# Sums over the partitions for sub-norm and modulation: ones stationary on four column groups and a turn, in place of one-column products

## The chip, the cores and the metric

The kernel runs on one core of a Trainium2 chip. The metric is the device time of one execution in microseconds (us): the median of three runs. Before the change it is 1350.98 us (the three runs span 1350.11 to 1352.2 us).

The engines have short names in all rows: PE is TensorE (PEld its loads of the stationary operand, which run ahead of the products), DVE is VectorE, ACT is ScalarE, POOL is GpSimd, SP is SyncE, which issues the DMA transfers. A PE product has a stationary operand (up to 128x128) and a moving operand whose columns stream through; its sum over the partitions lands in PSUM.

## The reference

The kernel computes two layers of a transformer block in float32 for 512 latent tokens `x` (width 1024), with 256 context tokens `ctx` that layer 0 reads. Cut to what matters here:

```python
for i in range(2):                                   # layer 0: diff_attention, layer 1: short_conv
    mod = silu(c) @ ada_w[i] + ada_b[i]              # (6*1024): "modulation"
    sh1, sc1, g1, sh2, sc2, g2 = split(mod, 6)
    h = rmsnorm(x, norm1_g[i]) * (1 + sc1) + sh1
    x = x + g1 * mixer(h, hc)
    x = x + g2 * swiglu(rmsnorm(x, norm2_g[i]) * (1 + sc2) + sh2)
return rmsnorm(x, final_g)
# swiglu(t) = (silu(a) * b) @ w_out,  a, b = split(t @ w_in), inner width 2816
# diff_attention: 8 heads; each head's output o (512 x 128) has a norm of its own, the "sub-norm":
o = o * rsqrt(mean(o * o, -1) + eps) * subln_g * (1 - lam_init)
```

Two quantities are sums over what the kernel keeps on the partitions. The sub-norm needs for every token the sum of o*o over the head's 128 values. The modulation needs, for each of its 12 parts of 1024 values (six per layer), the sum over 1024 inputs of silu(c) times a 1024x1024 block of `ada_w`.

## The kernel before

Activations are kept transposed, with the width on the partitions and the tokens along the free axis. A float32 product of full accuracy is made as three products of a reduced type, high by high, high by low and low by high (`mm3`, L79 to L81); `split` (L54 to L56) makes the two halves, the high one by a cast on ACT (L55), the low one by a subtraction on DVE (L56). Plain float32 products are used for the scores, the transposes and the sums; the trace records each of them as two passes on PE. A scheduler sets the order on each engine ahead of time from the program's order and its own idea of durations; on the chip each engine takes its instructions strictly in that order.

**Sub-norm** (`subnorm`, L547 to L566). For each head the squares `sq` (128x512) are summed over the partitions by four products (`pq`, L556) with a 128x128 block of `sq` stationary and one column of ones moving, so that the sums come out with the tokens on the partitions, one PSUM column for each 128 tokens. DVE and POOL make the scale from them, and `spread` (L196, tile `spro`) carries it back along the free axis. Head 7 does it in two halves of two products. `pq` takes one of the two PSUM buffers of the tag `pt`, which the transposed probabilities (`pt`, L532) and the head outputs (`po`) use too.

**Modulation** (`ada_steps`, L357 to L394). A part's 1024x1024 block is loaded as eight tiles `araw` of 512 KB into two buffers. DVE multiplies each by a scalar per partition and adds it into `ada` (L363 for the first, L365 for the other seven; `ada` has one buffer). What is left is a sum of `ada` (128x1024) over the partitions. The function is a generator: the program calls it a step at a time between pieces of other work. The first two of layer 0 are made at the start in another way, which the change leaves alone. Three parts are run in the attention with `spread_sum` off: eight one-column products each (`pada`, L372). Seven parts are run in the FFN of layer 0 with `spread_sum` on: `ada` is split on ACT and DVE into `adah` and `adal`, which take the two `araw` buffers; two pairs of 512-column products with a full block of ones stationary (L385) put the sum on all partitions; DVE picks the diagonal by a product with the identity, written back into `ada` (L387), and reduces it (L392). Such a part has 11 steps.

**FFN of layer 0** (`ffn_in`, L766 on). A step of its loop over the inner width is 48 products of 512 columns (`pa` and `pb`, three times eight each) on two loaded weight tiles `raw_f` of 512 KB; behind each step the program calls four steps of the modulation (`next(extra)`). `araw` and `raw_f` are issued from the same in-order queue, SP's.

**The output product of the attention**, with `da_wo`, has 120 products named `poa` for the first heads, which the schedule lays between the work of heads 6 and 7 where PE has nothing better.

Of the kernel before, what the change touches and what calls it, by code (L numbers as in the profile page):

```python
# [11 lines left out]
F32 = mybir.dt.float32  # L12
F32R = mybir.dt.float32r
AF = mybir.ActivationFunctionType
ALU = mybir.AluOpType
AX = mybir.AxisListType
PSUM = bass.MemoryType.PSUM

P = 128
EPS = 1e-6  # L20
# [5 lines left out]
def block_kernel(  # L26
# [11 lines left out]
    nc = tc.nc  # L38
    T = x.shape[1]
    C = ctx.shape[1]  # L40
    D = x.shape[2]
    F = ffn_w_out.shape[1]
    DB, FB, TB, CB = D // P, F // P, T // P, C // P
# [10 lines left out]
    def split(hi, lo, src):  # L54
        nc.scalar.copy(hi, src)  # L55
        nc.vector.tensor_tensor(lo, src, hi.bitcast(F32), op=ALU.subtract)  # L56
# [38 lines left out]
    ident = const.tile([P, P], F32, name="ident")  # L95
    make_identity(nc, ident)
    ones_f = const.tile([P, P], F32, name="ones_f")
    nc.vector.memset(ones_f, 1.0)
    ones_r = const.tile([P, P], F32R, name="ones_r")
# [12 lines left out]
    psB = tc.alloc_tile_pool(name="psB", bufs=2, space=PSUM)  # L112
# [9 lines left out]
    for tag, n, bufs in (  # L122
        [(f"Or{h}", 512, 1) for h in range(NH)] + [("qs0", 1024, 2), ("qs1", 1024, 2)]
        + [("e", 768, 3), ("pth", 768, 3), ("ptl", 768, 3), ("ks0", 768, 2), ("ks1", 768, 2)]
        + [(f"v{p}{t}", 256, 2) for t in range(KB) for p in "hl"]
        + [("sq", 512, 1), ("dg1", 512, 1)]
        + [(t, 4, 2) for t in ("sv", "sr", "rh", "rl")] + [(t, 4, 3) for t in ("rr", "mx")] + [("ss", 8, 2), ("den", 8, 2)]
        + [("ld", 2, 1)]
        + [("araw", 1024, 2), ("ada", 1024, 1), ("qt", 1024, 1), ("kt", 1536, 1), ("rcos", 512, 1), ("rsin", 512, 1)]
        + [("sw", 512, 1), ("rt", 512, 2)]  # L130
    ):
        ap.tile([P, n], F32, tag=tag, bufs=bufs, name=f"place_{tag}")
# [59 lines left out]
    def spread(r, n, tag, name):  # L192

        ps = psB.tile([P, 512], F32, tag=tag, name=f"spr{name}")[:, :n * P]
        for t in range(n):
            nc.tensor.transpose(ps[:, t * P:(t + 1) * P], r[:, t:t + 1].to_broadcast([P, P]), ident)  # L196
        return ps
# [62 lines left out]
    for k in range(0, DB, 2):  # L260
        pt = psB.tile([P, 2, T], F32, tag="S", name=f"ptx{k}")
# [9 lines left out]
    for i in range(2):  # L271
        pt = psB.tile([P, 4, C], F32, tag="S", name=f"ptc{i}")
        for a in range(4):
            k = 4 * i + a
# [62 lines left out]
    adab = [V1[:, 16:64], V2[:, 0:48]]  # L337
# [17 lines left out]
    def ada_steps(l, j, pool, ps_pool, spread_sum):  # L355

        acc = pool.tile([P, D], F32, tag="ada", bufs=1, name=f"ada{l}_{j}")  # L357
        for k in range(DB):
            raw = pool.tile([P, D], F32, tag="araw", name=f"araw{l}_{j}_{k}")
            nc.sync.dma_start(raw, ada_w[l, k * P:(k + 1) * P, j * D:(j + 1) * D])  # L360
            s = sil[:, 0, k:k + 1]
            if k == 0:
                nc.vector.tensor_scalar(acc, raw, s, None, op0=ALU.mult)  # L363
            else:
                nc.vector.scalar_tensor_tensor(acc, raw, s, acc, op0=ALU.mult, op1=ALU.add)  # L365
            if k < DB - 1:
                yield
        m = mod[l][:, 8 * j:8 * j + 8]
        if not spread_sum:
            ps = ps_pool.tile([P, 512], F32, tag="acc", name=f"pada{l}_{j}")[:, :DB]  # L370
            for k in range(DB):
                nc.tensor.matmul(  # L372
                    ps[:, k:k + 1], acc[:, k * P:(k + 1) * P], ones_f[:, 0:1], start=True, stop=True
                )
            nc.vector.tensor_tensor(m, ps, adab[l][:, 8 * j:8 * j + 8], op=ALU.add)
            yield
            return

        hi, lo = (pool.tile([P, D], F32R, tag="araw", name=f"ada{n}{l}_{j}") for n in "hl")
        split(hi, lo, acc)  # L380
        yield
        for hf in range(2):
            ps = ps_pool.tile([P, 512], F32, tag="pada", bufs=1, name=f"pada{l}_{j}_{hf}")
            for i, w in enumerate((hi, lo)):
                nc.tensor.matmul(ps, ones_r, w[:, hf * 512:(hf + 1) * 512], start=(i == 0), stop=(i == 1))  # L385
            d = acc[:, hf * 512:(hf + 1) * 512].rearrange("p (a b) -> p a b", b=P)
            nc.vector.tensor_tensor(  # L387
                d, ps.rearrange("p (a b) -> p a b", b=P), ident[:, None, :].to_broadcast([P, 4, P]),
                op=ALU.mult,
            )  # L390
            yield
        nc.vector.reduce_sum(out=m, in_=acc.rearrange("p (a b) -> p a b", b=P), axis=AX.X)  # L392
        nc.vector.tensor_tensor(m, m, adab[l][:, 8 * j:8 * j + 8], op=ALU.add)
        yield  # L394

    def steps(*gens):
# [94 lines left out]
    def attend(h, between, after=None):  # L491
# [53 lines left out]
        if not after:  # L545
            later.append(subnorm(h, den, 0, TB))

    def subnorm(h, den, t0, t1):

        n = t1 - t0  # L550
        O = On[h][:, t0 * P:t1 * P]
        sq = ap.tile([P, T], F32, tag="sq", bufs=1, name=f"sq{h}")[:, :n * P]
        nc.scalar.activation(sq, O, AF.Square)
        ps = psB.tile([P, 512], F32, tag="pt", name=f"pq{h}")[:, :n]
        for t in range(n):
            nc.tensor.matmul(  # L556
                ps[:, t:t + 1], sq[:, t * P:(t + 1) * P], ones_f[:, 0:1], start=True, stop=True
            )
        v = ap.tile([P, 4], F32, tag="sv", name=f"sv{h}")[:, :n]
        nc.vector.tensor_tensor(v, den[:, 0, t0:t1], den[:, 0, t0:t1], op=ALU.mult)  # L560
        nc.vector.scalar_tensor_tensor(v, v, EPS * P, ps, op0=ALU.mult, op1=ALU.add)
        r = ap.tile([P, 4], F32, tag="sr", name=f"sr{h}")[:, :n]
        nc.gpsimd.tensor_tensor(r, v, mhalf[:, :n], op=ALU.pow)
        yield
        rs = spread(r, n, "pt", f"o{h}_{t0}")
        nc.vector.scalar_tensor_tensor(O, O, gsub, rs, op0=ALU.mult, op1=ALU.mult)  # L566
# [3 lines left out]
    Q[0] = finish_q(0, qps)  # L570
    K[0] = finish_k(0, kps, kcps)
    adas = steps(*(ada_steps(0, j, ap, psB, False) for j in (2, 3, 4)))

    def norm_half(pool, ps_pool, l, A, jsh, dst, a, b, on_pe=False):
# [91 lines left out]
    for h in range(NH):  # L666
# [11 lines left out]
        def last(pr, den):  # L678
            if pr == 0:
                for i in range(NA, h):  # L680
                    split(O[i][0], O[i][1], On[i])

            def run():
                yield from subnorm(h, den, 2 * pr, 2 * pr + 2)
                a, b = halves[pr]
                split(O[h][0][:, a:b], O[h][1][:, a:b], On[h][:, a:b])

            later.append(run())
            if pr:
# [46 lines left out]
    xt_pool, op = pools  # L736
# [56 lines left out]
    def new_u(pool, l, n):  # L793
# [24 lines left out]
    for k in range(DB):  # L818
# [10 lines left out]
        v = lp.tile([P, T], F32, tag="t0", name="cv")  # L829
# [112 lines left out]
```

## Time and profile before

| | before |
|---|---|
| median of three runs | 1350.98 us (1350.11 to 1352.2) |
| profiled execution | 1350.57 us, span 1348.8 us |
| PE busy | 1302.2 us, 97% of the span |
| DVE, ACT, POOL busy | 58%, 37%, 7% of the span |
| sub-norm sums | 166 to 400 us, in the attention |
| modulation with spread_sum off | three parts, 128 to 284 us |
| modulation with spread_sum on | seven parts, 440 to 690 us, in layer 0's FFN |

The span is what the profile of one execution covers, from the first to the last instruction; the execution's own time is 1.8 us longer. A busy PE counts matmuls in flight, whose ends are modelled; where products follow one another without a gap, the spacing of their starts is the price of one.

### The profile page before, as it was taken

How to read it: one execution, taken by the hardware profiler on the slowest of the kernel's cores; microseconds unless marked ns; L12 is line 12 of the kernel's file. 1: busy time of each engine (PE TensorE's matmuls, PEld its weight loads, DVE VectorE, ACT ScalarE, POOL GpSimd, SP SyncE). 2: the span in 40 equal slices, each digit the busy share in tenths (PEclk: the TensorE clock that was granted, in tenths of full speed). 3: DMA queues.
4: the chain of work that ended last, by engine and by line, in shares of the span. 5: the costliest groups of instructions: out<-in, count | busy, mean ns of one | idle time of the engine just before them, and what ended most of it. 6: DMA issues, size and time to landing. Idle time of an engine off the chain costs nothing.

```text
span 1348.8 us, 17927 instructions
## 1 busy us (share of the span) xinstructions
PE 1302.2 (97%) x7068; PEld 1120.1 (83%) x7068; DVE 786.4 (58%) x1089; ACT 501.8 (37%) x841; POOL 97.2 (7%) x103
## 2 busy tenths in 40 slices
PE   6788999999999999999999999999999999999997
PEld 5568899999789888888788899888898888888887
DVE  6787989888867677767642265444563333332222
ACT  7534455545556333322222253222452223222122
POOL 2100000000014000000000050000420000000000
PEclk9998999999999999999999999999999999999999
DMA  9865755623532677667633323333233333333321
GB/s 301 259 202 146 207 126 172 156 64 96 153 110 84 184 218 218 207 214 218 210 102 102 101 65 110 94 102 101 79 94 94 99 104 94 94 91 113 100 72 63
DMA packets 238742, 182.79 MB, mean 136 GB/s; under 512 B 6937, under 2 KB 220226, under 8 KB 238658
## 3 DMA queue, kind: packets, MB, share of 16 engines
q1 hardware_dynamic: 238658, 181.65, 45.6%
q8 instruction: 55, 0.90, 0.3%
q14 instruction: 29, 0.24, 0.1%
HBM read 162.75 MB, written 4.19 MB: 124 GB/s over the span
## 4 chain that ended last, share of the span: by engine, by line
PE 82%; DMA 9%; DVE 5%; ACT 2%; issue 1%; SPq 1%; POOL 1%; DVEq 0%; ACTq 0%; POOLq 0%
PE po_fo L81 6%; PE po_fo L79 6%; PE po_fo L80 6%; DMA araw<-in_ada_w_dram 5%; PE pb L80 5%; PE pb L79 5%; PE pb L81 5%; PE pa L80 5%; PE pa L79 5%; PE pa L81 5%; PE S L511 3%; DMA raw_a<-in_ada_w_dram 2%; DVE ada L365 2%; PE pt L532 1%; PE psv L80 1%; PE psv L81 1%
## 5 line engine op out<-in xcount | busy, mean ns | idle before, releaser
L55 ACT CAST whi_f<-raw_f 128x1024 fp32r<-128x1024 f32 x87 | 91.4, 1051 | 232.7 <-issue 118.2
L56 DVE TENSOR_TENSOR wlo_f<-raw_f,whi_f 128x1024 fp32r<-128x1024 f32 x87 | 107.4, 1234 | 77.9 <-ACT whi_f L55 75.0
L56 DVE TENSOR_TENSOR wlo_fo<-raw_fo,whi_fo 128x1024 fp32r<-128x1024 f32 (+1 forms) x48 | 54.5, 1135 | 118.2 <-ACT whi_fo L55 116.8
L79 PE MATMUL po_fo<-uh,whi_fo 128*128 128x512 f32 (+1 forms) x324 | 118.7, 366 | 0.1
L80 PE MATMUL po_fo<-ul,whi_fo 128*128 128x512 f32 (+1 forms) x324 | 118.6, 366 | 0.0
L81 PE MATMUL po_fo<-uh,wlo_fo 128*128 128x512 f32 (+1 forms) x324 | 118.4, 365 | 0.0
L365 DVE SCALAR_TENSOR_TENSOR ada<-araw,sil,ada 128x1024 f32<-128x1024 f32 x70 | 90.1, 1287 | 47.4 <-DMA araw<-in_ada_w_dram 47.2
L55 ACT CAST whi_fo<-raw_fo 128x1024 fp32r<-128x1024 f32 (+1 forms) x48 | 47.1, 981 | 177.6 <-PE po_fo L80 142.3
L784 DVE TENSOR_TENSOR uu<-sl,pb 128x512 f32<-128x512 f32 (+1 forms) x48 | 30.7, 640 | 81.2 <-PE pb L81 76.7
L81 PE MATMUL pb<-h2h,wlo_f 128*128 128x512 f32 (+1 forms) x192 | 71.7, 374 | 0.0
L79 PE MATMUL pa<-h3h,whi_f 128*128 128x512 f32 (+1 forms) x192 | 71.5, 373 | 0.0
L80 PE MATMUL pb<-h2l,whi_f 128*128 128x512 f32 (+1 forms) x192 | 71.4, 372 | 0.0
L79 PE MATMUL pb<-h2h,whi_f 128*128 128x512 f32 (+1 forms) x192 | 71.4, 372 | 0.0
L81 PE MATMUL pb<-h3h,wlo_f 128*128 128x512 f32 (+1 forms) x192 | 71.3, 371 | 0.0
L80 PE MATMUL pb<-h3l,whi_f 128*128 128x512 f32 (+1 forms) x192 | 71.3, 371 | 0.0
L79 PE MATMUL pb<-h3h,whi_f 128*128 128x512 f32 (+1 forms) x192 | 71.3, 371 | 0.0
L81 PE MATMUL pa<-h3h,wlo_f 128*128 128x512 f32 (+1 forms) x192 | 71.3, 371 | 0.0
L80 PE MATMUL pa<-h3l,whi_f 128*128 128x512 f32 (+1 forms) x192 | 71.1, 371 | 0.0
L79 PEld LDWEIGHTS po_fo<-uh,whi_fo 128*128 128x128 f32 x324 | 61.1, 189 | 10.4 <-DVE on L871 0.3
L80 PEld LDWEIGHTS po_fo<-ul,whi_fo 128*128 128x128 f32 x324 | 61.1, 189 | 10.0
L81 PEld LDWEIGHTS po_fo<-uh,wlo_fo 128*128 128x128 f32 x324 | 61.1, 189 | 9.7
L519 ACT ACTIVATE e<-S,mx 128x768 f32<-128x768 f32 x64 | 58.1, 908 | 23.8 <-DVE mx L515 17.9
(337 smaller groups left out, 3462.9 us busy)
## 6 DMA issues: line engine op xcount, KB each, us to landing
raw_f<-in_ffn_w_in_dram SPq DMA_DIRECT2D x88, 512.0 KB, 3.7
araw<-in_ada_w_dram SPq DMA_DIRECT2D x80, 512.0 KB, 4.4
raw_fo<-in_ffn_w_out_dram SPq DMA_DIRECT2D x32, 512.0 KB, 3.6
raw_a<-in_ada_w_dram SPq DMA_DIRECT2D x32, 256.0 KB, 4.6
qs<-qt SPq DMA_DIRECT2D x32, 256.0 KB, 5.0
raw_wv<-in_da_wqkv_dram SPq DMA_DIRECT2D x12, 512.0 KB, 3.3
ks<-kt SPq DMA_DIRECT2D x32, 192.0 KB, 5.0
raw_fo<-in_ffn_w_out_dram SPq DMA_DIRECT2D x16, 384.0 KB, 3.2
```

Of the source, the lines that this page charges most:

```text
L55: nc.scalar.copy(hi, src)
L56: nc.vector.tensor_tensor(lo, src, hi.bitcast(F32), op=ALU.subtract)
L79: nc.tensor.matmul(ps, sh, mh, start=start, stop=False)
L80: nc.tensor.matmul(ps, sh, ml, start=False, stop=False)
L81: nc.tensor.matmul(ps, sl, mh, start=False, stop=stop)
L365: nc.vector.scalar_tensor_tensor(acc, raw, s, acc, op0=ALU.mult, op1=ALU.add)
L511: nc.tensor.matmul(S[:, a:b], q[m][:, j, qb * P:(qb + 1) * P], ks[m][:, a:b], start=(j == 0), stop=(j == 1),)
L519: nc.scalar.activation(em, S[:, :KV], AF.Exp, bias=mx[:, m:m + 1], accum_out=den[:, m, qb:qb + 1])
L532: nc.tensor.transpose(pt[:, i * P:(i + 1) * P], e[0][:, k * P:(k + 1) * P], ident)
L784: nc.vector.tensor_tensor(u, s, pb, op=ALU.mult)
```

## The change

The sums are made the other way round. A block of 32 columns of ones is stationary and the data move. Four products, one for each quarter of the data, write the PSUM partitions 0 to 31, 32 to 63, 64 to 95 and 96 to 127, so each uses another group of 32 columns of PE's array. ACT copies the result (128x128 for the sub-norm, 128x256 for the modulation) to SBUF, PE turns it (one transpose, or two), and DVE reads every 32nd column. For the sub-norm the scale's formula is otherwise as before; for the modulation both branches are replaced by this one, and a part in the FFN has 8 steps in place of 11, without `adah`, `adal`, the diagonal and the reduction.

```diff
         m = mod[l][:, 8 * j:8 * j + 8]
-        if not spread_sum:
-            ps = ps_pool.tile([P, 512], F32, tag="acc", name=f"pada{l}_{j}")[:, :DB]
-            for k in range(DB):
-                nc.tensor.matmul(
-                    ps[:, k:k + 1], acc[:, k * P:(k + 1) * P], ones_f[:, 0:1], start=True, stop=True
-                )
-            nc.vector.tensor_tensor(m, ps, adab[l][:, 8 * j:8 * j + 8], op=ALU.add)
-            yield
-            return
-
-        hi, lo = (pool.tile([P, D], F32R, tag="araw", name=f"ada{n}{l}_{j}") for n in "hl")
-        split(hi, lo, acc)
-        yield
-        for hf in range(2):
-            ps = ps_pool.tile([P, 512], F32, tag="pada", bufs=1, name=f"pada{l}_{j}_{hf}")
-            for i, w in enumerate((hi, lo)):
-                nc.tensor.matmul(ps, ones_r, w[:, hf * 512:(hf + 1) * 512], start=(i == 0), stop=(i == 1))
...
-            yield
-        nc.vector.reduce_sum(out=m, in_=acc.rearrange("p (a b) -> p a b", b=P), axis=AX.X)
-        nc.vector.tensor_tensor(m, m, adab[l][:, 8 * j:8 * j + 8], op=ALU.add)
+        ps = ps_pool.tile([P, 512], F32, tag="pada" if spread_sum else "acc",
+                          bufs=1 if spread_sum else None, name=f"pada{l}_{j}")
+        for g in range(4):
+            nc.tensor.matmul(
+                ps[32 * g:32 * g + 32, 0:256], ones_f[:, 0:32], acc[:, g * 256:(g + 1) * 256],
+                start=True, stop=True,
+            )
+        sums = pool.tile([P, 256], F32, tag="dg1", bufs=1, name=f"sada{l}_{j}")
+        nc.scalar.copy(sums, ps[:, 0:256])
+        for n in range(2):
+            nc.tensor.transpose(ps[:, 256 + n * P:256 + (n + 1) * P], sums[:, n * P:(n + 1) * P], ident)
+        nc.vector.tensor_tensor(
+            m.rearrange("p (g n) -> p g n", n=2),
+            ps[:, 256:512].rearrange("p (n g q) -> p n g q", n=2, q=32)[:, :, :, 0],
+            adab[l][:, 8 * j:8 * j + 8].rearrange("p (g n) -> p g n", n=2), op=ALU.add,
+        )
         yield
...
-        ps = psB.tile([P, 512], F32, tag="pt", name=f"pq{h}")[:, :n]
+        ps = psB.tile([P, 512], F32, tag="pt", name=f"pq{h}")
         for t in range(n):
             nc.tensor.matmul(
-                ps[:, t:t + 1], sq[:, t * P:(t + 1) * P], ones_f[:, 0:1], start=True, stop=True
+                ps[32 * t:32 * t + 32, 0:P], ones_f[:, 0:32], sq[:, t * P:(t + 1) * P], start=True, stop=True
             )
+        sums = ap.tile([P, P], F32, tag="sums", bufs=1, name=f"sums{h}")
+        nc.scalar.copy(sums[:32 * n], ps[:32 * n, 0:P])
+        pq = ps[:, P:P + 32 * n]
+        nc.tensor.transpose(pq, sums[:32 * n], ident[:32 * n, :32 * n])
```

In the built program the change also moves work. The first place is DVE in the FFN of layer 0, at the end of the modulation part 1_0 and the start of part 1_1. `uu`, `ul` and `wlo` belong to the FFN's own steps, `ada` and `mod` to the modulation. Before:

```order
L365 SCALAR_TENSOR_TENSOR ada1_0_5268<-araw1_0_7_5426,sil_197,ada1_0_5268 128x1024
L56 TENSOR_TENSOR wlo_f0_0_8_5601<-raw_f0_0_8_5598,whi_f0_0_8_5600 128x1024
L56 TENSOR_TENSOR adal1_0_5430<-ada1_0_5268,adah1_0_5429 128x1024
L784 TENSOR_TENSOR uu_5501<-sl_5499,pb6_5474 128x512
L56 TENSOR_TENSOR wlo_f2816_0_8_5607<-raw_f2816_0_8_5604,whi_f2816_0_8_5606 128x1024
L56 TENSOR_TENSOR ul0_6_4828<-uu_5501,uh0_6_4827 128x512
L387 TENSOR_TENSOR ada1_0_5268<-pada1_0_0_5433,ident_61 128x512
L56 TENSOR_TENSOR wlo_f0_0_9_5687<-raw_f0_0_9_5684,whi_f0_0_9_5686 128x1024
L387 TENSOR_TENSOR ada1_0_5268<-pada1_0_1_5505,ident_61 128x512
L392 TENSOR_REDUCE mod1_205<-ada1_0_5268 128x8
L393 TENSOR_TENSOR mod1_205<-mod1_205,V2_1002 128x8
L363 TENSOR_SCALAR ada1_1_5511<-araw1_1_0_5512,sil_197 128x1024
```

The same place of the changed kernel, from the last addition of part 1_0 on:

```order
L365 SCALAR_TENSOR_TENSOR ada1_0_5292<-araw1_0_7_5382,sil_198,ada1_0_5292 128x1024
L783 TENSOR_TENSOR uu_5369<-sl_5367,pb4_5342 128x512
L56 TENSOR_TENSOR wlo_f2816_0_6_5485<-raw_f2816_0_6_5482,whi_f2816_0_6_5484 128x1024
L56 TENSOR_TENSOR ul0_4_4852<-uu_5369,uh0_4_4851 128x512
L363 TENSOR_SCALAR ada1_1_5463<-araw1_1_0_5464,sil_198 128x1024
L365 SCALAR_TENSOR_TENSOR ada1_1_5463<-araw1_1_1_5467,sil_198,ada1_1_5463 128x1024
L365 SCALAR_TENSOR_TENSOR ada1_1_5463<-araw1_1_2_5470,sil_198,ada1_1_5463 128x1024
L56 TENSOR_TENSOR wlo_f0_0_7_5569<-raw_f0_0_7_5566,whi_f0_0_7_5568 128x1024
L382 TENSOR_TENSOR mod1_206<-pada1_0_5385,V2_1003 128x8
L365 SCALAR_TENSOR_TENSOR ada1_1_5463<-araw1_1_3_5473,sil_198,ada1_1_5463 128x1024
L365 SCALAR_TENSOR_TENSOR ada1_1_5463<-araw1_1_4_5544,sil_198,ada1_1_5463 128x1024
L783 TENSOR_TENSOR uu_5459<-sl_5457,pb5_5432 128x512
```

The next part's additions moved up: one `uu` (one FFN step) stands between the two parts' additions in both, but where `adal`, two L387 and L392 stood there are now additions of the next part, and two FFN steps hold a whole part. On PE, accordingly, exactly 96 FFN products stand between one part's `pada` and the next in each of the six gaps (142 to 154 of them before).

The second place is PE at one of those parts in the changed kernel, the sum of part 1_0 inside `pa5`; `pada` reads the finished `ada1_0`:

```order
L80 MATMUL pa5_5407<-h2l3_4156,whi_f0_0_5_5397 128x512
L374 MATMUL pada1_0_5385<-ada1_0_5292,ones_f_66 32x256 x4
L81 MATMUL pa5_5407<-h2h3_4155,wlo_f0_0_5_5398 128x512
L79 MATMUL pa5_5407<-h2h4_4157,whi_f0_0_5_5397 128x512
...
L80 MATMUL pb5_5432<-h2l2_4154,whi_f2816_0_5_5403 128x512
L381 MATMUL pada1_0_5385<-ident_61,sada1_0_5390 128x128 x2
L81 MATMUL pb5_5432<-h2h2_4153,wlo_f2816_0_5_5404 128x512
```

The four sums stand in one piece in the midst of FFN products, and the two turns 21 products behind them.

The third place is PE in the attention's last head, around the first half of its sub-norm (`pq7`); `pt` are the transposed probabilities of the next query blocks, `pob` an output product. Before:

```order
L81 MATMUL pob1_0_4499<-o6_4016,wlo_wob6_4478 128x256
L556 MATMUL pq7_4262<-ones_f_66,sq7_4260 128x1 x2
L532 MATMUL pt7_2_0_4295<-ident_61,e7_2_0_4281 128x128 x3
L532 MATMUL pt7_2_1_4301<-ident_61,e7_2_0_4281 128x128 x3
L196 MATMUL spro7_0_4307<-ident_61,sr7_4268 128x128 x2
L532 MATMUL pt7_3_0_4334<-ident_61,e7_3_0_4320 128x128 x3
```

And in the changed kernel:

```order
L81 MATMUL pob1_0_4527<-o6_4035,wlo_wob6_4506 128x256
L549 MATMUL pq7_4284<-sq7_4282,ones_f_66 32x128 x2
L525 MATMUL pt7_2_0_4320<-ident_61,e7_2_0_4306 128x128 x3
L555 MATMUL pq7_4284<-ident_61,sums7_4287 128x64
L525 MATMUL pt7_2_1_4326<-ident_61,e7_2_0_4306 128x128 x3
L196 MATMUL spro7_0_4332<-ident_61,sr7_4293 128x128 x2
```

The turn is new, three transposes behind its sums, and the products behind it wait where it waits. The 120 `poa` products also shifted: 75 of them stand ahead of head 7's first scores, where 26 stood before.

## Rows read from the trace of the kernel before

**Rows 1.** The profile's page: busy time by engine, and PE's granted clock in 40 slices.

```profile
PE 1302.2 (97%) x7068; PEld 1120.1 (83%) x7068; DVE 786.4 (58%) x1089; ACT 501.8 (37%) x841; POOL 97.2 (7%) x103
...
PEclk9998999999999999999999999999999999999999
```

**Rows 2.** Windows: length, then PE, PEld, DVE, ACT, POOL busy, PEclk, DMA share, GB/s.

```profile
256.00:290.00 34.00, 34.00 (x256) 32.26 (x255) 25.33 (x48) 18.36 (x39) 1.65 (x1) 1.00 0.33 84
350.00:404.00 54.00, 52.18 (x326) 45.82 (x327) 39.27 (x67) 28.35 (x56) 5.34 (x8) 1.00 0.34 103
475.00:500.00 25.00, 25.00 (x112) 20.70 (x111) 19.03 (x19) 9.10 (x11) 0.00 (x0) 1.00 0.77 237
440.00:575.00 135.00, 135.00 (x606) 111.85 (x606) 94.76 (x103) 45.05 (x58) 0.00 (x0) 1.00 0.67 207
```

**Rows 3.** Chain of waits: start us, us until the next piece, what (passes).

```profile
128.22 1.46 PE pada L372 x14
143.88 0.66 PE pt L532 x6
166.47 0.79 PE pq L556 x8
421.43 0.86 PE pn L586 x4
646.28 0.49 PE pada L385 x2
```

**Rows 4.** Single lines, PE: duration ns min/median/max, first and last start us, count.

```profile
L556 PE MATMUL pq<-ones_f,sq x64: 164/250/271, 166.3 to 400.3; 128*128 128x1 f32 x64
L372 PE MATMUL pada<-ones_f,ada x48: 166/250/250, 128.1 to 283.8; 128*128 128x1 f32 x48
```

**Rows 5.** Timeline of PE inside an FFN step: start us, duration us.

```profile
635.98 0.39 PE L79 MATMUL pa<-h2h,whi_f 128*128 128x512 f32 x1
636.20 0.39 PE L80 MATMUL pa<-h2l,whi_f 128*128 128x512 f32 x1
```

**Rows 6.** Chain of waits through two modulation parts of the FFN.

```profile
612.97 4.76 DMA araw<-in_ada_w_dram
617.83 1.30 DVE ada L365
619.14 5.54 DMA araw<-in_ada_w_dram
...
626.08 4.16 DMA araw<-in_ada_w_dram
...
631.64 4.98 DMA araw<-in_ada_w_dram
...
636.72 1.30 DVE ada L365
638.03 1.06 ACT adah L55
...
646.99 4.73 DMA araw<-in_ada_w_dram
...
672.46 1.05 ACT adah L55
```

**Rows 7.** Waits, 436 to 690 us: us in total, times, longest.

```profile
DVE ada L365 <- DMA araw<-in_ada_w_dram: 43.2, 37, 3.4
...
PE pada L385 <- ACT adah L55: 1.5, 2, 0.9
```

**Rows 8.** DMA issues, 440 to 680 us (KB, median us to landing); `araw` over the span.

```profile
araw<-in_ada_w_dram SPq DMA_DIRECT2D x52, 512.0 KB, 4.6
raw_f<-in_ffn_w_in_dram SPq DMA_DIRECT2D x36, 512.0 KB, 5.3
...
DMA to landing us min/median/max: 3.4/4.4/6.3
```

**Rows 9.** Timeline of ACT: the nearest copy of 128x256 out of PSUM.

```profile
128.51 0.38 ACT L55 CAST vh<-psv 128x256 fp32r<-128x256 f32 x1
```

More of the change, by code (lines that the diff above doesn't have):

```diff
@@ L125, in block_kernel @@
         + [(f"v{p}{t}", 256, 2) for t in range(KB) for p in "hl"]
-        + [("sq", 512, 1), ("dg1", 512, 1)]
+        + [("sq", 512, 1), ("dg1", 256, 1), ("sums", 256, 1)]
         + [(t, 4, 2) for t in ("sv", "sr", "rh", "rl")] + [(t, 4, 3) for t in ("rr", "mx")] + [("ss", 8, 2), ("den", 8, 2)]
@@ L368, in ada_steps @@
         m = mod[l][:, 8 * j:8 * j + 8]
-        if not spread_sum:
-            ps = ps_pool.tile([P, 512], F32, tag="acc", name=f"pada{l}_{j}")[:, :DB]
-            for k in range(DB):
-                nc.tensor.matmul(
-                    ps[:, k:k + 1], acc[:, k * P:(k + 1) * P], ones_f[:, 0:1], start=True, stop=True
-                )
-            nc.vector.tensor_tensor(m, ps, adab[l][:, 8 * j:8 * j + 8], op=ALU.add)
-            yield
-            return
-        hi, lo = (pool.tile([P, D], F32R, tag="araw", name=f"ada{n}{l}_{j}") for n in "hl")
-        split(hi, lo, acc)
-        yield
-        for hf in range(2):
-            ps = ps_pool.tile([P, 512], F32, tag="pada", bufs=1, name=f"pada{l}_{j}_{hf}")
-            for i, w in enumerate((hi, lo)):
-                nc.tensor.matmul(ps, ones_r, w[:, hf * 512:(hf + 1) * 512], start=(i == 0), stop=(i == 1))
[L386 to L389, printed above, removed]
-            )
-            yield
-        nc.vector.reduce_sum(out=m, in_=acc.rearrange("p (a b) -> p a b", b=P), axis=AX.X)
-        nc.vector.tensor_tensor(m, m, adab[l][:, 8 * j:8 * j + 8], op=ALU.add)
+        ps = ps_pool.tile([P, 512], F32, tag="pada" if spread_sum else "acc",
[4 more added lines that the diff above has]
+                start=True, stop=True,
+            )
+        sums = pool.tile([P, 256], F32, tag="dg1", bufs=1, name=f"sada{l}_{j}")
[4 more added lines that the diff above has]
+            m.rearrange("p (g n) -> p g n", n=2),
+            ps[:, 256:512].rearrange("p (n g q) -> p g n q", n=2, q=32)[:, :, :, 0],
+            adab[l][:, 8 * j:8 * j + 8].rearrange("p (g n) -> p g n", n=2), op=ALU.add,
+        )
         yield
@@ L553, in subnorm @@
         nc.scalar.activation(sq, O, AF.Square)
-        ps = psB.tile([P, 512], F32, tag="pt", name=f"pq{h}")[:, :n]
+        ps = psB.tile([P, 512], F32, tag="pt", name=f"pq{h}")
         for t in range(n):
             nc.tensor.matmul(
-                ps[:, t:t + 1], sq[:, t * P:(t + 1) * P], ones_f[:, 0:1], start=True, stop=True
+                ps[32 * t:32 * t + 32, 0:P], ones_f[:, 0:32], sq[:, t * P:(t + 1) * P], start=True, stop=True
             )
+        sums = ap.tile([P, P], F32, tag="sums", bufs=1, name=f"sums{h}")
+        nc.scalar.copy(sums[:32 * n], ps[:32 * n, 0:P])
+        pq = ps[:, P:P + 32 * n]
+        nc.tensor.transpose(pq, sums[:32 * n], ident[:32 * n, :32 * n])
         v = ap.tile([P, 4], F32, tag="sv", name=f"sv{h}")[:, :n]
         nc.vector.tensor_tensor(v, den[:, 0, t0:t1], den[:, 0, t0:t1], op=ALU.mult)
-        nc.vector.scalar_tensor_tensor(v, v, EPS * P, ps, op0=ALU.mult, op1=ALU.add)
+        nc.vector.scalar_tensor_tensor(
+            v, v, EPS * P, pq.rearrange("p (t q) -> p t q", q=32)[:, :, 0], op0=ALU.mult, op1=ALU.add
+        )
         r = ap.tile([P, 4], F32, tag="sr", name=f"sr{h}")[:, :n]
```

## The prediction

> **What bounds the kernel now.** The page comes first: PE is busy 97% of the span, every other engine at most 58%, and its clock is granted at 9 or 10 tenths throughout [rows 1], the higher of its two levels (2.4 GHz). So PE's time is the kernel's time, and a microsecond that leaves PE counts unless PE then waits. The windows say where there is slack: in the modulation's stretch of the attention PE has none (34.00 of 34 us), in the attention's last head 1.8 of 54 us, in the FFN of layer 0 none (135.00 of 135), and there DMA is busy two thirds of the time at 207 GB/s, in its dense stretches 237 GB/s [rows 2]. No clock change is part of the sum.
>
> Prices are spacings in the chain of waits, not the durations of single products: a one-column pass is recorded at 250 ns [rows 4], but 8 passes in a row move the chain by 0.79 us and 14 by 1.46 us, 0.10 us each [rows 3]. In the same way a pass over 128 columns costs 0.66/6 = 0.11 us, one over 256 columns 0.86/4 = 0.215 us, a pair of L385 0.49 us [rows 3], and an FFN product about 0.227 us, the mean spacing of starts (two of them 0.22 us apart, recorded at 0.39 us each) [rows 5].
>
> **The attention: old sums out, new sums in.** 64 passes of sub-norm and 48 of modulation go [rows 4]: 64 x 0.099 + 48 x 0.104 = 11.3 us, all from a PE that has hardly any slack. In come seven groups of four 128-column products and two of two (sub-norm), and three groups of four 256-column products (modulation), each product two passes. What a group costs depends on whether products on different column groups run beside each other, which no row of before shows. The bounds in pass-times for a group of four: 8 if one after another, 2 if wholly beside each other. I take 5, where only the second pass of one product and the first of the next, which use different columns, run together; for a group of two the three figures are 4, 2 and 3. Sub-norm is then 41 passes x 0.11 = 4.5 us (7.0 to 2.0), modulation 15 x 0.215 = 3.2 us (5.2 to 1.3). The turns are ordinary transposes of two passes: seven of 0.22 and two of 64 columns at half that, plus six of 0.22 for the modulation, 3.1 us. Together 10.8 us in for 11.3 out: **-0.5 us** (+4.0 to -4.9).
>
> The pass prices above make one column nearly as dear as 128 columns [rows 3]. A rule of the Trainium skill would turn this term into a clearer gain: "TensorE: Matmul & The Clock Gate", section "Measured speedup vs the span model", gives 2.38 times for three column tiles of 512 columns; an estimate from it is some 3.2 times for four, 2.5 pass-times in place of my 5, and the attention's term would be -4.2 us, the whole sum about +8. No row of before shows it.
>
> **The FFN of layer 0: PE's own work.** 14 pairs of L385 (seven parts, two halves) at 0.49 us go, and the 1.5 us that PE waited for `adah` [rows 3, 7]: 8.4 us. Per part 5 x 0.215 + 0.44 = 1.52 us come in, seven parts 10.6 us (15.1 to 6.1). That is **+2.2 us** (+6.7 to -2.3). What leaves DVE and ACT (`adal`, the two products with the identity, the reduction, `adah`) I cost at nothing: PE hides it, and DVE's waits in these additions end with the DMA (43.2 us in 37 waits) [rows 7], so a freer DVE does not bring `ada` sooner.
>
> **The FFN: the wait.** A part has 8 steps in place of 11, so it fits in two FFN steps, and 96 FFN products stand between one `pada` and the next. That gives PE 96 x 0.227 = 21.8 us plus the part's own 1.52 us, 23.3 us, before it asks for the next finished `ada`. What feeds it is a chain through two buffers: a load lands, DVE adds it in, the buffer is free, the next load starts. One turn of it brings two of the eight loads, so a part needs four. Between the additions that began at 617.83 and 636.72 lie three turns, 6.30 us each [rows 6]: 1.30 us of addition, 4.2 to 5.5 us of landing, 0.1 us of issue. Two whole parts took 638.03 - 612.97 = 25.1 us and 672.46 - 646.99 = 25.5 us from the first load to the finished `ada` [rows 6]. With the median landing of that stretch, 4.6 us [rows 8], a turn is 6.0 us and a part 24.0 us. Before, this was harmless: between two chains PE had the rest of 2.75 FFN steps (the second began at 646.99, 34 us after the first), and PE waited twice [rows 7]. Now the loads of the next part start as soon as the buffers are free, chain joins chain, and the period is the chain's. I take 24.8 us, since more loads then fall together: eight `araw` and four `raw_f` of 0.524 MB in 25 us are 250 GB/s, above the dense windows of before (237 GB/s) [rows 2]. PE is then 24.8 - 23.3 = 1.5 us late at each of six parts, **+9.1 us**. The wait stands in PE's in-order queue with FFN products behind it, and nothing fills it. If the column groups run wholly together PE comes sooner and waits 2.2 us, 13.0 in all; one after another, 0.9 us and 5.3. So B, the FFN's sum, hardly depends on them: +11.3 us (+10.7 to +12.0).
>
> **The turns' own waits.** PE now asks ACT for a copy between the sums and the turn. The nearest copy takes 0.38 us [rows 9]. In the FFN the turns stand 21 products (4.8 us) behind and are covered; in heads 0 to 6 mostly too. In the last head only three transposes (0.66 us [rows 3]) cover a copy that may queue behind an exponential, `pt`'s buffer is held longer, and the `poa` products that filled PE's gaps are used up earlier. PE's idle time there is 1.8 us [rows 2]; that it doubles is my value, **+1.5 us** (0 to +4).
>
> Sum: -0.5 + 11.3 + 1.5 = +12.3 us on the profiled execution's 1350.57 us, **1363 us**; that execution lies 0.4 us under the median, which changes nothing.
>
> **The rivals.**
>
> 1. *Faster: the loads keep up and the groups run together.* The place is the first product of each `pada` in the FFN. If a part's chain takes no longer than 21.8 + 0.87 = 22.7 us, which means a landing of 22.7/4 - 1.4 = 4.25 us or less, there is no wait, and with the groups wholly side by side the sum is -4.9 - 2.3 + 1.5 = -5.7: 1345 us. For it: landings reach down to 3.4 us [rows 8]. Against: the median there is 4.6 us with fewer loads together [rows 8], and the chains shown ran at 4.9.
> 2. *The column groups bring nothing.* The products run one after another, and the array empties when the shape of the stationary operand changes: 0.39 - 0.23 = 0.16 us [rows 5], twice for each of twelve groups in the attention, 3.8 us. Then +4.0 + 3.8 + 12.0 + 3 = +22.8: 1373 us. For it: a pass over 128 columns costs as much as the old one [rows 3], and there are as many; against: nothing but that separate columns need not wait.
> 3. *Half side by side, and the loads keep up* (a landing of 4.4 us, the median of the whole span [rows 8]): -0.5 + 2.2 + 1.5 = +3.2: 1354 us.
> 4. *The loads get longer.* If `araw` lands in 5.3 us, as `raw_f` does in this stretch [rows 8], a turn takes 6.7 us, a part 26.8, and the six waits 21 us: -0.5 + 2.2 + 21 + 1.5 = +24: 1375 us.
>
> The drain in rival 2 also stands in the Trainium skill: "TensorEngine Tiling (Array Packing)", section "Key Properties", says that a change of tiling mode drains TensorE. By it the emptying comes with every group, even where the four run together: about +3.8 us in the attention by the row's price. No row of before shows a switch.
>
> **How the numbers follow.** The forecast (the chain sets the FFN's pace, whatever the columns do) has a chance of 0.50; its own range is 1356 (a chain of 24.0 us, -4.8, and a little more side by side) to 1370 us (25.8 us, +6). Rival 1 has 0.11, rival 2 0.14, rival 3 0.16, rival 4 0.09. A measurement here tells 0.2%, 2.7 us, from no change. Faster is rival 1 and a little of the forecast's low end with full side-by-side work, 0.12; half of rival 3 falls within 0.2%, 0.08; the rest, 0.80, is slower. The range 1352 to 1376 us leaves out rival 1 and the far sides of rivals 2 and 4, under 2 in 10.
>
> **What would show it.** In the changed profile: PE waiting in front of `pada` (L374) for DVE's `ada`, six times 1 to 3 us; `pada` to `pada` 24 to 26 us; `ada` waiting for `araw`, landings of 4.6 us or more; starts of the new products spaced by 0.2 to 0.25 us for 256 columns if half side by side, 0.43 if not, under 0.15 if wholly; in the last head PE waiting for ACT's copy in front of L555. I am wrong if the modulation parts pass without PE waiting (the chain is shorter than I read it), or if the attention's stretch grows or shrinks by more than 5 us.

## The result: 1366.8 us, and the profile after

The changed kernel takes 1366.76 us (median of four runs, 1363.21 to 1367.59) against 1351.01 us before: 1.0118 times as long, with an interval of 1.0098 to 1.0139, or 15.75 us more. The page of its profiled execution (span 1365.8 us), busy time and the shares of the chain that ended last:

```profile
PE 1308.3 (96%) x7101; PEld 1115.4 (82%) x7101; DVE 760.5 (56%) x1061; ACT 499.8 (37%) x853; POOL 96.7 (7%) x103
...
PE 75%; DMA 11%; DVE 8%; issue 2%; ACT 2%; SPq 1%; POOL 1%; DVEq 0%; ACTq 0%; POOLq 0%
```

PE's busy share fell against [rows 1], so part of the added time is waiting. The starts of a few products in the two traces place it:

| stretch | before | after | difference |
|---|---|---|---|
| start to the first score product | 108.0 | 110.1 | +2.1 |
| attention: to the first product of the next norm (`pn`) | 298.0 | 302.2 | +4.2 |
| layer 0's FFN: to the first product of the short convolution | 386.0 | 394.0 | +8.0 |
| layer 1: to the last transpose | 549.4 | 552.2 | +2.8 |

The first and the last row hold no changed code. Over all the kernels profiled below the first score product came at 107.7 to 110.5 us, and the last stretch took 549.4 to 552.2 us, so of these 4.9 us a good part is how one execution differs from another. In layer 1 the granted clock of after falls twice (0.96 and 0.86 in 800 to 820 us, 0.83 in 990 to 1000), in before never. What the change does stands in the two middle rows, with one reserve: a late start can be made up. `ffn_only` below has the attention of before, starts its scores at 110.0 us and yet ends the attention at 405.9, where before ends it at 406.0. In after it ends at 412.3, so the attention lost between 4.2 us (from the first score) and 6.3 us (from the start).

Windows of after, with the columns of [rows 2]: the last head, and the FFN's stretch that answers to 440 to 575.

```profile
385.00:390.00 5.00, 2.95 (x22) 2.10 (x22) 4.71 (x9) 3.40 (x9) 0.30 (x1) 0.95 0.16 43
390.00:395.00 5.00, 4.75 (x22) 4.15 (x21) 3.46 (x8) 1.99 (x4) 0.71 (x1) 0.50 0.16 61
446.00:581.00 135.00, 129.16 (x603) 103.76 (x602) 92.77 (x100) 39.43 (x55) 0.00 (x0) 0.99 0.79 255
```

The last head of before in the same windows:

```profile
385.00:390.00 5.00, 4.43 (x33) 3.95 (x32) 5.00 (x11) 3.27 (x7) 0.00 (x0) 1.00 0.23 67
390.00:395.00 5.00, 3.91 (x27) 2.74 (x25) 3.24 (x8) 2.51 (x7) 0.69 (x1) 1.00 0.93 299
```

In the FFN PE now idles 5.8 us of 135 where it idled none, and DMA moves 255 GB/s in place of 207. In the last head PE is busy 2.95 of 5 us (4.43 before), and in the next 5 us its clock is granted at half, the lower of its two levels (1.2 GHz); before it was granted in full.

Waits of after, 430 to 640 us (us in total, times, longest):

```profile
DVE ada L365 <- DMA araw<-in_ada_w_dram: 50.1, 35, 3.5
...
PEld pada L374 <- issue: 10.3, 6, 3.2
PE pada L374 <- DVE ada L365: 8.2, 6, 2.8
```

The row `PE pada L374 <- DVE ada L365` is the predicted wait: six parts, PE idle 8.2 us in front of the sums. The 10.3 us of the row above belong to PEld, the load of the ones, and begin while PE's product before is still in flight. At the longest of these waits, 2.8 us of idling, the granted clock fell as well, to 0.84 in 485 to 490 us and 0.81 in 490 to 495, which is 1.7 us of work at full speed. One of the six in PE's timeline of after (start, duration, idle time before):

```profile
584.11 0.39 PE L80 MATMUL pa<-h2l,whi_f 128*128 128x512 f32 x1
585.68 0.64 PE L374 MATMUL pada<-ada,ones_f 128*32 128x256 f32 x8 [1.18 <-DVE ada L365]
586.25 0.50 PE L81 MATMUL pa<-h2h,wlo_f 128*128 128x512 f32 x1
```

The next FFN product should have started at 584.34; PE stood until 585.68. The eight passes of the new sum then took 0.57 us together. The sums of the seven parts start at 462.9, 488.6, 513.0, 537.5, 561.6, 585.7 and 609.8 us, 24.5 us apart on average.

The chain of waits of after, through the middle of one part, answers to [rows 6]:

```profile
540.35 4.90 DMA araw<-in_ada_w_dram
...
545.34 1.30 DVE ada L365
546.65 3.96 DMA araw<-in_ada_w_dram
...
550.71 0.06 DVE ada L365
...
551.91 0.68 DVE uu L783
552.59 1.14 DVE wlo_f L56
553.73 0.60 DVE ul L56
554.33 1.29 DVE ada L365
555.63 4.47 DMA araw<-in_ada_w_dram
```

The load of 546.65 landed at 550.61 and was added at once, at 550.71. The next load, issued at 549.06, was added at 554.33, and DVE was not idle before that: it had the FFN's own `uu`, `wlo_f` and `ul` in its queue. Most additions still wait for the load and not for DVE: 35 of the 49 of L365, by the row of waits above (37 before [rows 7]). Landings (median us) of after, 440 to 640 us:

```profile
araw<-in_ada_w_dram SPq DMA_DIRECT2D x54, 512.0 KB, 4.0
raw_f<-in_ffn_w_in_dram SPq DMA_DIRECT2D x34, 512.0 KB, 4.9
```

The medians are those of the few loads whose landing the trace records (14 of the 54 `araw` here). By them the loads land sooner than in [rows 8] (4.0 against 4.6). From the issue of a load to its addition 4.9 us pass on average, in after and in before alike, so the loads did not get slower, although more of them fall together.

### The profile page after: what moved, and what is told of

The parts are those of the page before. It is cut to its first block, busy times and chain, and to the rows that moved or that the text cites. A ratio compares the mean times of both kernels' runs of the same rounds, so it can differ in the third digit from the quotient of the medians.

```text
span 1365.8 us, 17981 instructions
## 1 busy us (share of the span) xinstructions
PE 1308.3 (96%) x7101; PEld 1115.4 (82%) x7101; DVE 760.5 (56%) x1061; ACT 499.8 (37%) x853; POOL 96.7 (7%) x103
## 4 chain that ended last, share of the span: by engine, by line
PE 75%; DMA 11%; DVE 8%; issue 2%; ACT 2%; SPq 1%; POOL 1%; DVEq 0%; ACTq 0%; POOLq 0%
DMA araw<-in_ada_w_dram 9%; PE po_fo L79 6%; PE po_fo L80 6%; PE po_fo L81 6%; PE pb L79 4%; PE pb L80 4%; PE pb L81 4%; PE pa L81 4%; PE pa L79 4%; PE pa L80 4%; PE S L504 3%; DVE ada L365 2%; PE pt L525 1%; PE psv L79 1%; PE psv L80 1%
## 5 line engine op out<-in xcount | busy, mean ns | idle before, releaser
L365 DVE SCALAR_TENSOR_TENSOR ada<-araw,sil,ada 128x1024 f32<-128x1024 f32 x70 | 90.1, 1287 | 54.2 <-DMA araw<-in_ada_w_dram 54.0
L79 PEld LDWEIGHTS po_fo<-uh,whi_fo 128*128 128x128 f32 x324 | 61.1, 189 | 10.3 <-DVE on L870 0.3
L508 DVE TENSOR_REDUCE mx<-S 128x1 f32<-128x768 f32 x64 | 60.8, 951 | 14.6 <-PE S L504 14.5
## 6 DMA issues: line engine op xcount, KB each, us to landing
raw_fo<-in_ffn_w_out_dram SPq DMA_DIRECT2D x16, 384.0 KB, 3.3
```

The costliest lines, as they stand in the source:

```text
L79: nc.tensor.matmul(ps, sh, mh, start=start, stop=False)
L508: nc.vector.tensor_reduce(out=mx[:, m:m + 1], in_=S[:, :KV], axis=AX.X, op=ALU.max, negate=True)
```

## The experiments

Each kernel was timed beside the kernel before; ratios are to that, with the interval. All but `groups` were timed in five rounds. They were timed in several groups, in which the median of the kernel before lay between 1348.7 and 1352.5 us; a difference between two rows therefore goes by the ratios (0.0010 is 1.4 us).

| kernel | median us | ratio (interval) |
|---|---|---|
| `ffn_only` | 1359.14 | 1.0069 (1.0042 to 1.0095) |
| `subnorm_only` | 1355.45 | 1.0044 (1.0029 to 1.0058) |
| `attn_mod_only` | 1347.68 | 0.9976 (0.9961 to 0.9991) |
| `ffn_11_steps` | 1355.65 | 1.0038 (1.0024 to 1.0052) |
| `araw3` | 1354.62 | 1.0031 (1.0018 to 1.0043) |
| `mod_11_steps` | 1345.36 | 0.9962 (0.9949 to 0.9975) |
| `head7_old` | 1355.41 | 1.0040 (1.0027 to 1.0053) |
| `heads67_old` | 1354.72 | 1.0027 (1.0013 to 1.0040) |
| `pq_acc` | 1387.18 | 1.0279 (1.0254 to 1.0305) |
| `hold_filler` | 1353.46 | 1.0028 (1.0015 to 1.0040) |
| `hold_h67` | 1352.39 | 1.0028 (1.0014 to 1.0043) |
| `groups` | 1365.2 (one run) | |

**One part of the change at a time.** `ffn_only`, `subnorm_only` and `attn_mod_only` take the new form for one of the three places and the old code for the rest. In short, the first two:

```diff
--- ffn_only, from before
         m = mod[l][:, 8 * j:8 * j + 8]
         if not spread_sum:
...
             return
...
-        hi, lo = (pool.tile([P, D], F32R, tag="araw", name=f"ada{n}{l}_{j}") for n in "hl")
-        split(hi, lo, acc)
...
+        for g in range(4):
+            nc.tensor.matmul(
+                ps[32 * g:32 * g + 32, 0:256], ones_f[:, 0:32], acc[:, g * 256:(g + 1) * 256],
+                start=True, stop=True,
+            )
...
--- subnorm_only, from before
-                ps[:, t:t + 1], sq[:, t * P:(t + 1) * P], ones_f[:, 0:1], start=True, stop=True
+                ps[32 * t:32 * t + 32, 0:P], ones_f[:, 0:32], sq[:, t * P:(t + 1) * P], start=True, stop=True
...
```

> The kernel before with only the FFN's seven parts made in the new way; sub-norm and the attention's three parts as before. Theory W: +8 us over before, 1359, with PE waits of 1.3 to 3 us in front of six of the sums. Rival A (most of the 15.8 us stands in the attention): +3, 1354.

> The kernel before with only the sub-norm's sums made in the new way. Theory H (the copy and the turn stand in the path of the last head, where nothing covers them): the sums themselves save 2 to 3 us, the last head loses 5 to 7, together +3 to +5: 1354 to 1356. Rival F (the last head loses because its filler, the first heads' output products, has been used up earlier by the attention's modulation parts): -2, 1349.

> The kernel before with only the attention's three modulation parts made in the new way. Theory H: the sums cost 0.57 + 0.44 us a part in place of 1.67, nothing else changes: -2 us, 1349. Rival F: 60 of the filler's 120 products stand ahead of the last head's scores (26 before), the last head is left without cover: +3 to +5, 1354 to 1356.

The FFN part alone costs 8 us, as theory W has it, with the sums again 24.4 us apart. The sub-norm alone costs 4 us by the medians, 6 by the ratio. The attention's modulation alone gains 3.4 us: rival F's loss from the shifted filler did not come, with 60 of 120 filler products ahead of the last head. By the medians the three add up to 9 us, by the ratios to 12 (0.69 + 0.44 - 0.24 in a hundred), where the whole change costs 15.8 (13.2 to 18.8 by its interval). Whether the parts are worse together than apart is not clear of this noise.

**The wait in the FFN.** `ffn_11_steps` gives back the pace, `araw3` the loads:

```diff
--- ffn_11_steps, from after (at the end of a part)
+        if spread_sum:
+            for _ in range(3):
+                yield
--- araw3, from after
-            raw = pool.tile([P, D], F32, tag="araw", name=f"araw{l}_{j}_{k}")
+            raw = pool.tile([P, D], F32, tag="araw", bufs=3 if spread_sum else None, name=f"araw{l}_{j}_{k}")
```

> The changed kernel with three empty steps put behind each modulation part of the FFN, so that a part takes 11 steps again and 107 to 144 FFN products stand between one part's sum and the next, in place of 96. Theory W (the chain of loads is too slow for two FFN steps, and PE waits for it): PE's waits in front of the sums fall from about 10 us to under 2, the time falls by 8 to 10 us to about 1357. Rival T (the new sums, copies and turns themselves cost the time in the FFN): the waits may go but the time stays within 2 us of the changed kernel's 1367.

> The changed kernel (1366.8) with three buffers for the modulation's loads in the FFN in place of two, the order of PE's work unchanged at 96 products between sums. Theory W (two loads in flight set the period of 24.5 us): three in flight give about 16 to 18 us, PE's waits in front of the sums go, -9 to -11 us: 1356 to 1358. Rival D (the DMA queues are full, and more loads in flight only land later): within 3 us of 1366.8.

Both took the FFN's loss away: the kernels are 11.1 and 12.1 us faster than after, and the FFN's stretch of the table above takes 384.9 and 384.0 us (386.0 before, 394.0 after). In `ffn_11_steps` PE's waits for `ada` fall to 1.1 us in one place. Waits of `araw3`, 430 to 660 us, and landings, 440 to 640:

```profile
DVE ada L365 <- DMA araw<-in_ada_w_dram: 12.3, 16, 2.5
...
PEld pada L374 <- PE pb L80: 2.1, 6, 0.4
```

```profile
araw<-in_ada_w_dram SPq DMA_DIRECT2D x53, 512.0 KB, 5.5
raw_f<-in_ffn_w_in_dram SPq DMA_DIRECT2D x36, 512.0 KB, 3.7
```

A single load now takes longer (5.5 against 4.0 us), and yet PE no longer waits for `ada`, only for its own product before: with a third buffer the landing is no longer in the chain's period. The sums come 22.8 us apart, which is 96 products and the part's own 1.0 us and nothing else. Theory W stands, rivals T and D fall. One thing more shows in these stretches: `attn_mod_only` and `subnorm_only`, whose FFN makes its sums in the old way, need 384.0 and 384.2 us for it. With the pace kept, the new sums cost in the FFN what the old ones cost.

**The column groups.** `groups` issues a part's four products a second time, on four groups in even parts and all on the last group in odd ones.

```diff
+        for g in ((3, 3, 3, 3) if j % 2 else range(4)):
+            nc.tensor.matmul(
+                ps[32 * g:32 * g + 32, 0:256], ones_f[:, 0:32], acc[:, g * 256:(g + 1) * 256],
+                start=True, stop=True,
+            )
```

> As ffn_11_steps with every modulation part's four products issued again: in parts 0, 2 and 4 on the four column groups once more, in parts 1, 3 and 5 four times on the last group. Theory S (products on different column groups run wholly beside each other): the extra four cost about 0.45 us on four groups and 1.7 us on one (eight passes of 0.215). Rival P (only neighbouring passes overlap, and the 0.57 us seen in the changed kernel comes from something else): 1.1 us on four groups; 1.7 on one.

Its chain of waits, an even part and an odd one (L374 the first set, L379 the second):

```profile
497.92 0.57 PE pada L374 x8
498.49 0.43 PE pada L379 x8
...
532.10 0.57 PE pada L374 x8
532.67 1.73 PE pada L379 x8
```

Theory S, to the hundredth: eight more passes take 1.73 us on one group, 0.43 us on four.

**Where the attention loses.** `mod_11_steps` is the old sub-norm with all of the new modulation, `head7_old` and `heads67_old` have the old sums in the last head or the last two heads only (all with 11 steps).

```diff
--- mod_11_steps, from ffn_11_steps
-                ps[32 * t:32 * t + 32, 0:P], ones_f[:, 0:32], sq[:, t * P:(t + 1) * P], start=True, stop=True
+                ps[:, t:t + 1], sq[:, t * P:(t + 1) * P], ones_f[:, 0:1], start=True, stop=True
...
--- head7_old, from ffn_11_steps (heads67_old: h >= NH - 2)
+        if h == NH - 1:
+            ps = psB.tile([P, 512], F32, tag="pt", name=f"pq{h}")[:, :n]
+            for t in range(n):
+                nc.tensor.matmul(
+                    ps[:, t:t + 1], sq[:, t * P:(t + 1) * P], ones_f[:, 0:1], start=True, stop=True
+                )
+            pq = ps
+        else:
...
```

> Sub-norm as before, all modulation parts in the new way, eleven steps to a part in the FFN. Theories W and H together: the attention's saving (1347.7 was measured with it alone) and the FFN's own saving of 1 to 2 us add up, 1346 +- 2, which would be under both kernels. Rival T (the new sums cost what the old ones did in the FFN): 1348 to 1350.

> As ffn_11_steps (1355.7), but head 7's sub-norm, and that alone, made with the old one-column products; the other heads in the new way, and the filler stands as in the changed kernel (75 of 120 ahead of the last head's scores). Theory H (the copy and the turn in the last head's path cost the time there): -4 to -6 us, 1350 to 1352. Rival F (the filler is gone, the last head waits whichever way its sums are made): within 1.5 us of 1355.7.

> As ffn_11_steps (1355.7), with the sub-norm of heads 6 and 7 made with the old products, the new way for heads 0 to 5; 75 filler products still stand ahead of the last head's scores. Theory H2 (head 6's sub-norm, which runs inside the last head, is what hurts: its copy and turn hold a buffer of the transposes, PE idles and its granted clock falls): 1344 to 1348, at or under mod_11_steps (1345.4). Rival F (filler used up too early): 1353 or more, with the granted clock of the last head still falling.

`mod_11_steps` is the fastest kernel of the study, 5.5 us under the kernel before. Its interval overlaps that of `attn_mod_only` (0.9976), and its FFN takes 383.9 us where that one's takes 384.0; that the FFN's parts add to the gain is not shown. The other two fell on the rival's side: the old sums in the heads where the time is lost give back nothing (0.2 us) or hardly anything (0.9 us, 1.5 by the ratios, within the noise). So it is not head 7's or head 6's own copy and turn that cost most of it.

`pq_acc` puts the sums into the accumulators' buffers, `hold_filler` ties the last four of the filler's blocks to the last head's four query blocks, and `hold_h67` is `hold_filler` with `heads67_old`:

```diff
--- pq_acc, from ffn_11_steps
-        ps = psB.tile([P, 512], F32, tag="pt", name=f"pq{h}")
+        ps = psB.tile([P, 512], F32, tag="acc", name=f"pq{h}")
--- hold_filler, from ffn_11_steps (scores: the last head's score products in order, eight a block)
+    for n in (0, 8, 16, 24):
+        with tc.issue_after(scores[n]):
+            next(wo, None)
```

> As ffn_11_steps, with the sub-norm's sums and turn in a PSUM buffer of the accumulators (tag acc) in place of one of the two that the transposes use; the schedule then leaves 90 of 120 filler products for the last head (45 in the changed kernel). Theory H2 (the held buffer stops the transposes): PE no longer waits for DVE's read of the sums in front of a transpose, 1346 to 1350. Rival C (the chain of copy, turn and read is too long whichever buffer it holds): 1353 to 1356.

> As ffn_11_steps (1355.7), every head's sub-norm in the new way, but the last four of the filler's eight output blocks may be issued only behind the first score product of the last head's first, second, third and fourth query block: 60, 75, 90 and 105 of 120 filler products then stand ahead of the four blocks (75, 115, 120, 120 in ffn_11_steps; 26, 60, 90, 106 in the kernel before). Theory F (the sub-norm's change let the schedule use the filler up before the last head, which then idles and drops to the lower clock): 1346 to 1349, with no fall of the granted clock between 375 and 405 us. Theory H (the sums' copy, turn and read cost the time in the heads themselves): 1353 to 1356.

> Both remedies at once: the new sub-norm for heads 0 to 5 only (as heads67_old, 1354.7) and the filler held back (as hold_filler, 1353.5). Theory F+H2 (in the last head the filler and head 6's copy and turn share the loss, and each remedy alone left the other's): 1346 to 1349, PE's waits between 375 and 411 us down to the 4 to 5 us of mod_11_steps. Rival E (the loss comes earlier, from waits that the new sums or the shifted order make in the heads before, such as the 1.7 us at 333 us): 1351 to 1354.

`pq_acc` missed both expectations: 1387 us. The accumulators are what the next head's projections use, the order of the attention changed again, and PE's longest waits there are for the next head's keys (`S` for `ks`, three waits, 8.7 us in total, the longest 6.8). As a test of the held buffer it says little. `hold_filler` did what it was to do with the clock, but not with the time. Its windows in the last head:

```profile
385.00:390.00 5.00, 3.08 (x21) 2.51 (x22) 4.22 (x10) 2.80 (x7) 1.65 (x1) 1.00 0.80 245
390.00:395.00 5.00, 4.00 (x31) 3.09 (x30) 2.87 (x7) 2.19 (x6) 0.54 (x1) 1.00 0.53 173
```

The clock stays up where after had 0.50, and PE still idles as much between 385 and 390. By the ratios `hold_filler` and `hold_h67` gain 1.4 us each on `ffn_11_steps` (2.2 and 3.3 by the medians), which is not clear of noise; their times are those of theory H and of rival E. Most of the loss stands elsewhere. The trace of `hold_filler` shows one such place, ACT and PE at 332 to 336 us:

```profile
332.24 2.70 ACT L55 CAST o<-O 128x512 fp32r<-128x512 f32 x5
...
334.84 0.47 ACT L55 CAST pth<-pt 128x384 fp32r<-128x384 f32 x1
335.37 0.38 PE L79 MATMUL po<-pth,vh 128*128 128x256 f32 x1 [1.72 <-ACT pth L55]
```

Five casts that ready the filler's operands stand on ACT ahead of the one cast that PE waits for. The same wait of 1.7 us stands in after. Between 330 and 375 us PE was busy 41.48 of 45 us in `hold_filler`, and all of it in `mod_11_steps`:

```profile
330.00:375.00 45.00, 41.48 (x235) 34.62 (x235) 36.91 (x65) 24.06 (x51) 1.46 (x1) 1.00 0.42 122
```

```profile
330.00:375.00 45.00, 45.00 (x260) 39.18 (x259) 37.76 (x65) 24.55 (x49) 1.64 (x1) 1.00 0.51 144
```

The same windows for more kernels, as PE's idle time in us, beside the filler's place and the end of the attention (the first product of the next norm):

| kernel | filler ahead of the last head's four query blocks | idle 160 to 330 | 330 to 375 | 375 to 411 | attention ends |
|---|---|---|---|---|---|
| before | 26, 60, 90, 106 | 0.0 | 2.2 | 2.5 | 406.0 |
| `mod_11_steps` | 60, 77, 102, 120 | 1.0 | 0.0 | 3.9 | 403.4 |
| after | 75, 115, 120, 120 | 1.4 | 1.8 | 5.7 | 412.3 |
| `hold_filler` | 60, 75, 90, 105 | 1.4 | 3.5 | 4.8 | 408.6 |
| `hold_h67` | 60, 75, 90, 105 | 1.4 | 3.5 | 4.2 | 409.3 |

Two things follow. Holding the filler back moved PE's idle time to earlier heads and did not remove it: 9.8 us in all in `hold_filler`, 9.0 in after, 4.7 before. And `mod_11_steps` uses the filler up no later than `hold_filler` does, yet idles half as much, so the filler's place alone does not cost the time.

What stays open: `hold_h67` and `mod_11_steps` are 7 us apart and differ in the sub-norm of heads 0 to 5, whose new sums are cheaper by themselves, and in the order that comes with it. Most of the loss therefore comes with those six heads. Whether their own copies, turns and longer-held buffers make it, or the waits of other work that the new order brings (such as the one at 335 us), no run separated.

## Why the prediction was right, step by step

**The mechanism of the main term was right, and the sum was 3.4 us low**: +12.3 us forecast, +15.75 measured, inside the forecast's own range. By the table of stretches the FFN's term was 3.3 us too high (+11.3 for +8.0) and the attention's 3.2 to 5.3 us too low (+1.0 for +4.2 to +6.3), and some of what was measured stands where no code changed. That the sum came so near is in part luck.

**The chain of loads** was the main term and is shown: +9.1 us of waits forecast, 8.2 in the row (8.7 by the starts, against a sum for which PE does not wait), a period of 24.8 us forecast and 24.5 measured, and both remedies, one that gives the loads longer and one that lets more of them run, took the FFN's loss away. The size came out so near by some luck: the loads' period was 0.3 us shorter than I took it and PE's own need (22.8 us for my 23.3) 0.5 us shorter, and the two errors offset each other. The make-up of the period was not quite as I had it either. I took four turns of load and addition with longer landings, and gave landings of 4.6 us or more as a sign; the recorded ones have a median of 4.0, from issue to addition 4.9 us pass as before, and in part of the turns it is DVE's own FFN work that an addition stands behind (551.91 to 554.33 above).

**The FFN's own work** was forecast at +2.2 us: seven times 1.52 us. Measured where nothing waits (`araw3`) a part moves the FFN's products by 1.0 us, 0.78 for the sums and 0.23 for the turns, so 7.1 us for seven, against the 6.9 + 1.5 that left, so -1.3. With 8.7 us of waits and the 1.7 us at the lower clock that is +9.1 us, for the 11.3 forecast and the 8.0 of the table of stretches.

**The turns** I priced at two passes each. The scores and the transposes have one record a product, only the sums have two: the ten parts' twenty turns are twenty records.

```profile
L381 PE MATMUL pada<-ident,sada x20: 270/271/330, 132.8 to 615.4; 128*128 128x128 f32 x20
```

A turn thus costs 0.11 us and not 0.22, in the attention some 1.7 us in all for my 3.1. The description of the kernel before, which gives the scores and the transposes two passes, is wrong in this.

**The column groups** were mis-sized to the other side. I took 5 pass-times for a group, half side by side; it is 2, and the two changes of shape. In the attention a head's sums took 0.91 us of PE before; they take 0.56 now, and the turn 0.12. A modulation part took 1.7 us and takes 1.0. Together that is -3.3 us in place of -0.5, 1.2 of it in the sub-norm. The Trainium skill had this more nearly: "TensorE: Matmul & The Clock Gate", section "Measured speedup vs the span model", from which I had estimated 3.2 times for four; measured here 1.73/0.43 = 4.0 times for the passes themselves. The emptying at a change of tiling ("TensorEngine Tiling (Array Packing)", section "Key Properties") fits what is there too: 0.34 us a group, 0.09 ahead of the sums, 0.14 in the set and 0.11 on the product behind it, where rival 2 had twice 0.16.

**The turns' own waits**, the term for all new waits of the attention, are the step that failed in size: "that it doubles is my value, +1.5 us (0 to +4)". The attention grew by 4.2 to 6.3 us although its sums and turns shrank by 3.3, so 7.5 to 9.6 us were lost; the upper count of its growth is past the 5 us that I had named as a sign of being wrong. PE's idle time between 160 and 411 us went from 4.7 to 9.0, and the lower clock in 385 to 400 us (0.95, 0.50, 0.87) took up to 3.4 more; the rest I can't place. "No clock change is part of the sum" put at nothing a term that was not nothing.

The wait that I expected, for ACT's copy in front of the turn, came to 0.2 us; it was the transposes behind that waited, 1.5 us for DVE's read of the turned sums, which frees their buffer. I had named the used-up filler and the longer-held buffer and priced them by the idle time of the old order; but the sub-norm's change moved the order of everything around it. The runs show that the sub-norm brings the loss (`subnorm_only`, and `mod_11_steps` against `ffn_11_steps`, 10 us), that most of it is not the last two heads' sums, and that the filler's place alone is not its cause.

**The rivals.** Rivals 1 and 3 needed the loads to keep up; they do with a third buffer, and even then the kernel takes 1354.6 us and not 1345, because the attention's loss stays; that this is rival 3's time is chance, for its groups half side by side are not what `groups` shows. Rival 2 falls by `groups`, though its price for the emptying held. Rival 4 had longer landings; they were not longer.

One slice of [rows 1] reads 8 tenths of clock, not "9 or 10"; the sum does not rest on it.

## What to carry to other kernels

A step that is made shorter brings the next step's inputs due earlier: ask what period feeds it (here 24.5 us for eight loads through two buffers), and compare it with the period at which the faster step will ask (22.8 us). Sums over partitions with 32 columns of ones on four column groups are a good exchange in PE time against one-column products, where the copy and the turn have other work beside them. Here they pay in the attention's modulation (0.9976 by itself), are even with the old form in the FFN once the pace is kept, and do not pay in the sub-norm, where a head saves only 0.23 us of PE. Where a scheduler sets the order, a small change to one chain moves others, and its price can't be read from that chain alone.

## What the runs showed of the hardware

Products on four column groups start some 0.007 us after one another and take the time of one: 0.43 us for eight passes of 256 columns against 1.73 us on one group, and 0.34 us more a group for the two changes of shape. The lower clock can outlast the idling that came before it. PE's timeline of after in the last head, `po` products ahead of the idle stretch and behind it:

```profile
381.12 0.28 PE L80 MATMUL po<-ptl,vh 128*128 128x256 f32 x1
381.23 0.28 PE L81 MATMUL po<-pth,vl 128*128 128x256 f32 x1
...
389.61 0.90 PE L525 MATMUL pt<-ident,e 128*128 128x128 f32 x3 [1.28 <-DVE sv L558]
390.76 1.11 PE L196 MATMUL spro<-ident,sr 128*128 128x128 f32 x4 [0.25 <-POOL sr L562]
...
392.27 0.42 PE L81 MATMUL po<-pth,vl 128*128 128x256 f32 x1
392.49 0.41 PE L79 MATMUL po<-pth,vh 128*128 128x256 f32 x1
```

The starts are 0.12 us apart before, 0.21 us after, at a granted clock of 0.50: 18 products so, 1.6 us lost behind 2 us of idling between 385 and 390. And a load that lands later need not cost: with three buffers `araw` took 5.5 us in place of 4.0 where the landing is recorded, and the kernel was 12 us faster.
